# A two-layer decoder trunk in fp32: FFN in two parts with h kept in DRAM, and four gate and up groups with a fourth seven-product pair

## The chip, the cores and the metric

The kernel runs on one core of one Trainium2 chip. The metric is the device time of one execution in microseconds, the median of the runs. The engines are PE (matrix products), DVE (vector), ACT (scalar), POOL and SP; the last two mostly issue DMAs here, though POOL computes a little as well.

## What is computed

Two pre-norm residual layers on 256 rows of width 2048, in float32: the first mixes by sliding-window attention beside an mLSTM, the second by forgetting attention; each ends in a SwiGLU FFN of hidden width 5632. The change concerns the two FFNs alone.

```
def swiglu(xn, w_gate, w_up, w_down):
    return (jax.nn.silu(xn @ w_gate) * (xn @ w_up)) @ w_down

for layer in range(DEPTH):          # DEPTH = 2
    ...
    h = h + mix
    h = h + swiglu(rms_norm(h, norm_ffn[layer]), w_gate[layer], w_up[layer], w_down[layer])
return rms_norm(h, norm_final)
```

## The kernel before

**Products in three pieces.** Each float32 operand is split into a high and a low half of PE's faster 32-bit type. ACT casts the high half (L187, or L356 in `split_plain`), DVE subtracts it from the raw value for the low half (L188, L357). A product is three matmuls (`three`, L531 to L534, or `gemm`, L222 to L224): high by high, high by low, low by high. The right operand of a matmul is a 128x512 block of weights, the left a 128x128 block of the activations, which are kept turned (k on the partitions): `xh, xl` for the normed input, `mh, ml` for the FFN's middle values.

**Pairs of k tiles.** `pair_group` (L539) computes two 512-wide column blocks at once (gate and up, or two neighbouring blocks of down) over an order of k pairs. An entry (0, pair) is a plain pair: two matrices, two k tiles, two row tiles, three matmuls each. An entry (1, pair) is a block product in seven products instead of eight: DVE makes four differences of the weights (L607 to L610), they are split like weights, and the sums of the activations that go with them (`sums_of`, L263) have been made once beforehand. It holds four `prod` banks of PSUM beside the four plain `acc` banks; `combine` (L553) puts the four products together into the tile `c` (one buffer), to which the plain banks are added (L665). The two sets of banks come from two pools of four and change places from one group to the next (`par`).

**Orders.** `ORDER` makes pairs 1, 3 and 5 of the eight k pairs seven-product pairs. `HEAVY` makes it 1, 3, 5 and 7, and begins with pair 1; groups in `DENSE` use it, and `DENSE` is empty. The sums for pair 7 (`FOURTH`) are made all the same and lie in halves of `xh, xl` that seven-product pairs don't read, and in `x4`. `DOWN` has the orders for down, by number of k pairs.

**Stages.** FFN_HIDDEN is 11 groups of 512. `PARTS` = (0, 3, 7, 11) cuts them into three parts, of 3, 4 and 4 groups. In each part `ffn` (L637) runs its gate and up groups (silu at L667, the product with up at L669), and then the down products of that part's 12 or 16 k tiles, whose results are added to h in SBUF (L758, and `add_out`, L370). `mh, ml` hold the 16 k tiles of one part. In layer 1 the last part's second column half is computed plainly by `gemm`, with the final norm.

**Turning the middle values.** After a group, ACT separates c into 16-bit planes (L697) and SP turns them by transposing DMAs; `join`, which runs in place 5 or 6 of the next group's order, puts the planes together (L704), splits them and makes the sums for down. The last group of a part of three groups is turned by PE instead (L683), because its down run has no room to wait.

**What sets the order.** The tile framework schedules each engine's instructions from the order of emission, so neighbouring groups overlap. Converted weights go to a stock of eight buffer pairs (`slot`, L106), used in turn; raw weights come by SP's DMAs of 512 KB (L134) into four buffers for plain and four for seven-product pairs. h is a single buffer with the tag "h"; POOL issues the few DMAs that are not SP's.

Of the kernel before, what the change touches and what calls it, by code (L numbers as in the profile page):

```python
# [7 lines left out]
F32 = mybir.dt.float32  # L8
# [4 lines left out]
ALU = mybir.AluOpType  # L13
# [49 lines left out]
AHEAD_M = (1, 2)  # L63
PQ_AT = 6
TURNED_V = 2
PARTS = (0, 3, 7, 11)


def mixed_of(order):
# [6 lines left out]
def trunk(  # L76
# [459 lines left out]
    def bank(par, name):  # L536
        return pm.tile([P, NB], F32, tag="pm", name=name) if par else pa.tile([P, NB], F32, tag="acc", name=name)
# [99 lines left out]
    def ffn(layer, fp, sx, x4, sd, key, todo, idx_next=None, key_next=None, finish=None):  # L637
        r = rstd(key)

        def sums_x(pair):  # L640
# [2 lines left out]
            j = mixed_of(ORDER).index(pair)  # L643
            return four(sx[0], j), four(sx[1], j)

        for g0, g1 in zip(PARTS, PARTS[1:]):
            end = g1 == PARTS[-1]
            nk = 4 * (g1 - g0)
            order = DOWN[nk // 2]
            for g in range(g0, g1):  # L650
# [17 lines left out]
                for t in range(NT):  # L668
# [5 lines left out]
                        op0=ALU.mult,  # L674
                        op1=ALU.mult,
                    )
                if g == g1 - 1 and nk < 16:
                    for half in range(2):
                        pt = bank(par, "pf").rearrange("p (i q) -> p i q", i=2)
                        for i in range(2):  # L680
                            cs = (2 * half + i) * P
                            for t in range(NT):
                                nc.tensor.transpose(pt[:, i, t * P : (t + 1) * P], c[:, t, cs : cs + P], ident)  # L683
                        pair = 2 * (g - g0) + half
                        k = 2 * pair
                        split_plain(mh[:, k : k + 2, :], ml[:, k : k + 2, :], pt)
                        if pair in mixed_of(order):
                            j = mixed_of(order).index(pair)
                            sums_of(
                                fp, sd[0][:, j, :, :], sd[1][:, j, :, :], lambda full, pt=pt: nc.scalar.copy(full, pt)  # L690
                            )
# [8 lines left out]
                def join(c=c, turned=turned, g=g, g0=g0, order=order):  # L700
# [4 lines left out]
                    k = 4 * (g - g0)  # L705
                    split_plain(
                        mh[:, k : k + 4, :].rearrange("p k s -> p (k s)"), ml[:, k : k + 4, :].rearrange("p k s -> p (k s)"), ct
                    )
                    for half in range(2):
                        pair = 2 * (g - g0) + half  # L710
                        if pair in mixed_of(order):
                            j = mixed_of(order).index(pair)
                            sums_of(
                                fp,
                                sd[0][:, j, :, :],
                                sd[1][:, j, :, :],
                                None,
                                ct[:, half * 512 : (half + 1) * 512].rearrange("p (i t q) -> p i t q", i=2, t=NT),
                            )

                todo = [(MID if g < g1 - 1 else MID_DOWN, join)]

            def sums_d(pair, order=order):
                j = mixed_of(order).index(pair)
                return four(sd[0], j), four(sd[1], j)

            def close(acc, n):
                if not end:
                    add_out(acc, n)
                elif idx_next is None:  # L730
                    finish(acc, n, gf)
                else:
                    add_out(acc, n)
                    if n < 1:
                        todo.append((LATER_DOWN[n], split_turned(idx_next, n, *scrap(fp, n))))
                    else:
                        split_scaled(idx_next, n)
                    square_sum(key_next, n)

            gf = None  # L740
            wd = w_down[layer][4 * g0 * P : 4 * g1 * P, :]
            for n0 in (0, 2):
                if end and idx_next is None and n0 == 2:
                    for n in (2, 3):
                        acc = new_acc()
                        gemm(acc, m_of, wd, n * NB, NB, 0, nk, nk, skew=3 if n == 3 else 1, halved=n == 3)
# [6 lines left out]
                if end and idx_next is None:  # L753
                    gf = fp.tile([P, D], F32, tag="c", name="gf", bufs=1)
                    nc.gpsimd.dma_start(gf, norm_final.partition_broadcast(P))
                for t in range(NT):
                    o = h[:, t, n0 * NB : (n0 + 2) * NB]
                    nc.vector.tensor_tensor(  # L758
                        out=o, in0=c[:, 2 * t : 2 * t + 2, :].rearrange("p a n -> p (a n)"), in1=o, op=ALU.add
                    )  # L760
                for m in range(2):
                    close(plain[m], n0 + m)

    def close_layer(layer, w_out, idx, key, **rest):
        with tc.tile_pool(name=f"fp{layer}", bufs=2) as fp:
            nx = len(mixed_of(ORDER))
            nd = max(len(mixed_of(o)) for o in DOWN.values())
            sx = [fp.tile([P, nx, 4, P], F32R, name=f"sx{i}", bufs=1) for i in range(2)]
# [608 lines left out]
```

## Time and profile before

| | |
|---|---|
| runs | 2077.94, 2077.02, 2076.69 us, median 2077.02 |
| profiled execution | 2077.56 us, span 2075.9 us, clock 0.999 |
| PE | 2065.7 us busy, 9473 instructions |
| DVE | 1819.0 us busy, 2367 instructions |
| ACT | 1373.7 us busy |
| DMA | 209 GB/s on average, 408.68 MB read from HBM |
| first silu of layer 0, of layer 1 | at 365.4 us, at 1422.6 us |

Times in views of the trace are counted from the span's start. A busy row is the union of an engine's instructions; one that waits is not busy. In the groups' lists a line gives code line, engine, operation, out<-in and shape. In a list of waits a row names who waited, for whom, the total, the number of times and the longest.

### The profile page before, as it was taken

The numbers are of one execution on the slowest core, as the hardware profiler recorded it, in microseconds if no ns is written. First come the engines' busy times: TensorE is split into PE (matmuls) and PEld (weight loads), VectorE is DVE, ScalarE is ACT, GpSimd is POOL, SyncE is SP. The second block draws the span as 40 slices with busy tenths as digits, with TensorE's granted clock in tenths as the row PEclk, the third lists the DMA queues.
The fourth block names the chain that finished last, engine by engine and source line by source line (L and its number), as shares of the span: only waits on it lengthen the run. The fifth ranks groups of instructions, "written<-read, shape, count | busy, mean of one in ns | idle before, by whom it ended". The sixth has DMA issues, their size and how long they took to land.

```text
span 2075.9 us, 26965 instructions
## 1 busy us (share of the span) xinstructions
PE 2065.7 (100%) x9473; PEld 1715.1 (83%) x9473; DVE 1819.0 (88%) x2367; ACT 1373.7 (66%) x1744; POOL 44.6 (2%) x66
## 2 busy tenths in 40 slices
PE   9999999999999999999999999999999999999998
PEld 7878888888888888888888888888888888888886
DVE  6788769999999999999899688689999999999994
ACT  6777678664676656667676776687655666556763
POOL 1010000000000000000000001000000000000000
PEclk9999999999999999999999999999999999999999
DMA  8566577666677666766676776586756677667764
GB/s 292 169 216 192 188 244 238 206 219 196 210 223 224 193 208 217 222 204 183 206 213 209 231 201 183 155 268 217 233 187 218 209 217 224 202 195 225 206 196 141
DMA packets 309576, 434.88 MB, mean 209 GB/s; under 512 B 106412, under 2 KB 114624, under 8 KB 309312
## 3 DMA queue, kind: packets, MB, share of 16 engines
q1 hardware_dynamic: 307088, 426.27, 66.1%
q0 software_dynamic: 1632, 5.80, 0.8%
q8 instruction: 74, 1.21, 0.2%
q10 hardware_dynamic: 720, 1.09, 0.2%
q14 instruction: 62, 0.51, 0.1%
HBM read 408.68 MB, written 2.12 MB: 198 GB/s over the span
## 4 chain that ended last, share of the span: by engine, by line
PE 97%; DVE 1%; ACT 1%; issue 1%; DMA 0%; POOLq 0%; POOL 0%; ACTq 0%; DVEq 0%
PE acc L532 21%; PE acc L534 21%; PE acc L533 21%; PE acc L223 6%; PE acc L222 6%; PE acc L224 6%; PE prod L532 5%; PE prod L533 5%; PE prod L534 5%; PE p L386 1%; PE po L487 1%; ACT s L420 0%; PE po L488 0%; DVE lo L188 0%; DMA raw<-in_w_down_dram 0%
## 5 line engine op out<-in xcount | busy, mean ns | idle before, releaser
L188 DVE TENSOR_TENSOR lo<-raw,hi 128x1024 fp32r<-128x1024 f32 (+3 forms) x656 | 771.1, 1195 | 135.5 <-ACT hi L187 133.0
L187 ACT CAST hi<-raw 128x1024 fp32r<-128x1024 f32 (+3 forms) x656 | 661.7, 1027 | 341.2 <-PE acc L534 137.2
L533 PE MATMUL acc<-lo,xh 128*128 128x512 f32 x1320 | 514.0, 389 | 0.0
L534 PE MATMUL acc<-hi,xl 128*128 128x512 f32 x1320 | 511.4, 389 | 0.0
L532 PE MATMUL acc<-hi,xh 128*128 128x512 f32 x1320 | 506.2, 390 | 0.0
L534 PEld LDWEIGHTS acc<-hi,xl 128*128 128x128 f32 x1320 | 247.8, 188 | 51.6
L533 PEld LDWEIGHTS acc<-lo,xh 128*128 128x128 f32 x1320 | 247.8, 188 | 51.4 <-issue 0.2
L532 PEld LDWEIGHTS acc<-hi,xh 128*128 128x128 f32 x1320 | 247.7, 188 | 51.3 <-issue 0.2
L356 ACT CAST hi<-raw 128x512 fp32r<-128x512 f32 x204 | 166.9, 819 | 160.7 <-PE acc L534 83.6
L357 DVE TENSOR_TENSOR lo<-raw,hi 128x512 fp32r<-128x512 f32 x204 | 191.6, 939 | 11.4 <-ACT hi L356 10.4
L533 PE MATMUL acc<-lo,mh 128*128 128x512 f32 x466 | 181.0, 389 | 0.0
L534 PE MATMUL acc<-hi,ml 128*128 128x512 f32 x466 | 180.3, 389 | 0.0
L532 PE MATMUL acc<-hi,mh 128*128 128x512 f32 x466 | 176.2, 389 | 0.1
L356 ACT CAST hi<-t 128x1024 fp32r<-128x1024 f32 x95 | 100.0, 1053 | 63.9 <-PE acc L534 38.0
L357 DVE TENSOR_TENSOR lo<-t,hi 128x1024 fp32r<-128x1024 f32 x95 | 116.2, 1224 | 15.2 <-ACT hi L356 15.0
L223 PE MATMUL acc<-lo,mh 128*128 128x512 f32 (+1 forms) x322 | 126.3, 392 | 0.0
L222 PE MATMUL acc<-hi,mh 128*128 128x512 f32 (+1 forms) x322 | 125.8, 391 | 0.0
L224 PE MATMUL acc<-hi,ml 128*128 128x512 f32 (+1 forms) x322 | 123.7, 391 | 0.0
L532 PEld LDWEIGHTS acc<-hi,mh 128*128 128x128 f32 x466 | 87.5, 188 | 18.5 <-ACT hi L187 0.5
L534 PEld LDWEIGHTS acc<-hi,ml 128*128 128x128 f32 x466 | 87.5, 188 | 18.2
L533 PEld LDWEIGHTS acc<-lo,mh 128*128 128x128 f32 x466 | 87.4, 188 | 18.2
L223 PE MATMUL acc<-lo,xh 128*128 128x512 f32 (+3 forms) x288 | 100.0, 348 | 0.2 <-DVE lo L188 0.2
(356 smaller groups left out, 3174.7 us busy)
## 6 DMA issues: line engine op xcount, KB each, us to landing
raw<-in_w_gate_dram SPq DMA_DIRECT2D x176, 512.0 KB, 4.5
raw<-in_w_up_dram SPq DMA_DIRECT2D x176, 512.0 KB, 4.6
raw<-in_w_down_dram SPq DMA_DIRECT2D x176, 512.0 KB, 4.8
raw<-in_w_in_odd_dram SPq DMA_DIRECT2D x88, 512.0 KB, 5.3
raw<-in_w_in_even_dram SPq DMA_DIRECT2D x51, 512.0 KB, 5.1
raw<-in_w_out_even_dram SPq DMA_DIRECT2D x32, 512.0 KB, 5.2
raw<-in_w_out_odd_dram SPq DMA_DIRECT2D x32, 512.0 KB, 4.7
hr<-in_w_in_even_dram SPq DMA_DIRECT2D x12, 512.0 KB, 4.5
```

The lines of the kernel that those rows point to most:

```text
L187: latest[0] = nc.scalar.copy(hi[:, k, 0:n], raw[:, k, 0:n])
L188: nc.vector.tensor_tensor(out=lo[:, k, 0:n], in0=raw[:, k, 0:n], in1=hi[:, k, 0:n].bitcast(F32), op=ALU.subtract)
L222: nc.tensor.matmul(o, ah[:, ts], hi, start=(k == 0), stop=False)
L223: nc.tensor.matmul(o, ah[:, ts], lo, start=False, stop=False)
L224: nc.tensor.matmul(o, al[:, ts], hi, start=False, stop=(k == k_all - 1 and cs.stop == n))
L356: nc.scalar.copy(dst_h, src)
L357: nc.vector.tensor_tensor(out=dst_l, in0=src, in1=dst_h.bitcast(F32), op=ALU.subtract)
L386: nc.tensor.matmul(pq[j % 2][:, j // 2, :], q_of(j, b), k_of(j)[:, 0:cols], start=True, stop=True)
L487: nc.tensor.matmul(po, v_of(j, 0), tt[:, j, 0:2, :].rearrange("p c q -> p (c q)"), start=True, stop=False)
L532: nc.tensor.matmul(o, ah, hi, start=start, stop=False)
L533: nc.tensor.matmul(o, ah, lo, start=False, stop=False)
L534: nc.tensor.matmul(o, al, hi, start=False, stop=stop)
```

## The change

`PARTS` becomes (0, 6, 11): two parts of 6 and 5 groups, so down runs over 12 and 10 pairs, each order with four seven-product pairs (1, 3, 5, 7 and 1, 3, 5, 8). `DENSE` becomes (3, 5, 7, 9). The first part has 24 k tiles of middle values, eight more than `mh, ml` hold. They go where h lay: h is stored to a DRAM tile `kept` as ffn begins, the tile `more` takes its SBUF buffer, and the first part's down results are added to `kept` by accumulating DMAs from c, issued by POOL. When the second part begins, h is loaded back. The second part's four extra k tiles go into the buffers `sx0, sx1`, free by then. The sums of the fourth down pair lie in halves that are not read otherwise. All groups are turned by DMA, and L683 is gone. `par` now simply alternates.

```
-DENSE = ()
+NK2 = 8
+DENSE = (3, 5, 7, 9)
 DOWN = {
-    6: ((0, 0), (1, 1), (0, 2), (1, 3), (0, 4), (0, 5)),
-    8: ((0, 0), (1, 1), (0, 2), (1, 3), (0, 4), (1, 5), (0, 6), (0, 7)),
+    12: tuple((int(pair in (1, 3, 5, 7)), pair) for pair in range(12)),
+    10: tuple((int(pair in (1, 3, 5, 8)), pair) for pair in range(10)),
 }
+DOWN_FOURTH = {12: 7, 10: 8}
-PARTS = (0, 3, 7, 11)
+PARTS = (0, 6, 11)
...
+        nonlocal h
+        par = 1
+        kept = dp.tile([P, NT, D], F32, name=f"kept{layer}")
+        for cs in (slice(0, D // 2), slice(D // 2, D)):
+            nc.gpsimd.dma_start(kept[:, :, cs], h[:, :, cs])
+        over = None
+        def mid(k, n):
+            if k < KT:
+                return mh[:, k : k + n, :], ml[:, k : k + n, :]
+            return tuple(m[:, k - KT : k - KT + n, :] for m in over)
...
+            if end:
+                h = cp.tile([P, NT, D], F32, tag="h", name="h")
+                for cs in (slice(0, D // 2), slice(D // 2, D)):
+                    nc.gpsimd.dma_start(h[:, :, cs], kept[:, :, cs])
+            else:
+                more = cp.tile([P, 2, NK2, S], F32R, tag="h", name="more")
+                over = more[:, 0, :, :], more[:, 1, :, :]
+            def room_of(pair, order=order, fourth=fourth, end=end):
+                if pair != fourth:
+                    j = mixed_of(order).index(pair)
+                    return sd[0][:, j, :, :], sd[1][:, j, :, :]
+                if end:
+                    return tuple(m[:, 4:6, :].rearrange("p a (b q) -> p (a b) q", b=2) for m in over)
+                return mh[:, 2:15:4, P:S], ml[:, 2:15:4, P:S]
             for g in range(g0, g1):
-                par = (g1 - 1 - g) % 2
+                par = 1 - par
...
-                if g == g1 - 1 and nk < 16:
-                    for half in range(2):
-                        pt = bank(par, "pf").rearrange("p (i q) -> p i q", i=2)
...
-                                nc.tensor.transpose(pt[:, i, t * P : (t + 1) * P], c[:, t, cs : cs + P], ident)
...
-                    continue
...
+            if end:
+                over = [fp.tile([P, 6, S], F32R, tag=f"sx{i}", name=f"over{i}", bufs=1) for i in range(2)]
...
             for n0 in (0, 2):
...
+                par = 1 - par
                 plain, c = pair_group(
-                    fp, 1 - n0 // 2, m_of, sums_d, [(wd, n0 * NB), (wd, (n0 + 1) * NB)], order, todo
+                    fp, par, mid_of, sums_d, [(wd, n0 * NB), (wd, (n0 + 1) * NB)], order, todo
                 )
+                if not end:
+                    for m in range(2):
+                        for t in range(NT):
+                            o = c[:, 2 * t + m, :]
+                            nc.vector.tensor_tensor(out=o, in0=plain[m][t], in1=o, op=ALU.add)
+                    nc.gpsimd.dma_start(
+                        kept[:, :, n0 * NB : (n0 + 2) * NB],
+                        c.rearrange("p (t m) n -> p t (m n)", t=NT),
+                        accum_op=ALU.add,
+                    )
+                    continue
```

More of the change, by code (lines that the diff above doesn't have):

```diff
@@ L699, in ffn, with join @@
                         nc.sync.dma_start_transpose(turned[b][:, :, t, :], flat[:, b, t, :])
-                def join(c=c, turned=turned, g=g, g0=g0, order=order):
+                def join(c=c, turned=turned, k=4 * (g - g0), order=order, room_of=room_of):
                     ct = c[:, 0:2, :].rearrange("p a n -> p (a n)")
@@ L704, in join @@
                         nc.scalar.copy(cb[:, :, b], turned[b].rearrange("p k t q -> p (k t q)"))
[L705 to L708, printed above, removed]
+                    split_plain(*(m.rearrange("p k s -> p (k s)") for m in mid(k, 4)), ct)
                     for half in range(2):
-                        pair = 2 * (g - g0) + half
+                        pair = k // 2 + half
                         if pair in mixed_of(order):
-                            j = mixed_of(order).index(pair)
                             sums_of(
                                 fp,
-                                sd[0][:, j, :, :],
-                                sd[1][:, j, :, :],
+                                *room_of(pair),
                                 None,
@@ L721, in ffn, with sums_d @@
                 todo = [(MID if g < g1 - 1 else MID_DOWN, join)]
-            def sums_d(pair, order=order):
-                j = mixed_of(order).index(pair)
-                return four(sd[0], j), four(sd[1], j)
+            if end:
+                over = [fp.tile([P, 6, S], F32R, tag=f"sx{i}", name=f"over{i}", bufs=1) for i in range(2)]
+            def sums_d(pair, room_of=room_of):
+                return [[m[:, e, :] for e in range(4)] for m in room_of(pair)]
             def close(acc, n):
-                if not end:
-                    add_out(acc, n)
-                elif idx_next is None:
+                if idx_next is None:
                     finish(acc, n, gf)
-                else:
[L733 to L738, printed above, removed]
+                    return
+                add_out(acc, n)
+                if n < 1:
+                    todo.append((LATER_DOWN[n], split_turned(idx_next, n, *scrap(fp, n))))
+                else:
+                    split_scaled(idx_next, n)
+                square_sum(key_next, n)
             gf = None
```

22 lines of the change are left out of this document (7 added, 15 removed).

## The prediction

> **What bounds the kernel now.** I read the page's first two parts and its chain, then who waited for whom on PE, then the order of time around one part boundary, then busy times group by group.
>
> ```profile
> PE 2065.7 (100%) x9473; PEld 1715.1 (83%) x9473; DVE 1819.0 (88%) x2367; ACT 1373.7 (66%) x1744; POOL 44.6 (2%) x66
> ...
> DVE  6788769999999999999899688689999999999994
> ...
> PE 97%; DVE 1%; ACT 1%; issue 1%; DMA 0%; POOLq 0%; POOL 0%; ACTq 0%; DVEq 0%
> ```
> ```profile
> PE cold L170 <- POOL ones L167: 1.2, 1, 1.2
> PE acc L223 <- DVE lo L188: 0.2, 1, 0.2
> PE acc L222 <- ACT hi L785: 0.2, 1, 0.2
> ```
>
> The reader is to see that PE works for 2065.7 of 2075.9 us, that the chain that ended last is 97% PE, and that all its waits for other engines come to 1.6 us. So PE alone sets the time: an instruction taken from PE is worth its full pace, as long as the engines that feed it keep ahead. VectorE (DVE) is the one that may not: its digits stand at 9 in both FFNs (slices 6 to 17 and the last ten), where it makes the low halves of the weights and the differences for the seven-product pairs.
>
> **What one matmul is worth.** A busy PE row is no price, because matmuls overlap (389 ns each, by the groups). The price is the distance between starts. From the order of time on PE at the end of the first down run of layer 0:
>
> ```profile
> 455.68 0.39 PE L533 MATMUL acc<-lo,mh 128*128 128x512 f32 x1
> ...
> 460.44 0.39 PE L534 MATMUL acc<-hi,ml 128*128 128x512 f32 x1
> 460.67 0.38 PE L683 MATMUL pf<-ident,c 128*128 128x128 f32 x2
> 460.81 0.48 PE L532 MATMUL prod<-hi,mh 128*128 128x512 f32 x1
> 461.12 0.39 PE L533 MATMUL prod<-lo,mh 128*128 128x512 f32 x1
> ```
>
> Between the first two rows lie 21 steps: 4.76 / 21 = 0.2267 us per 128x512 matmul. From 460.67 to 461.12 stand two transposes and one matmul: (0.45 - 0.227) / 2 = 0.11 us per transpose.
>
> The Trainium skill (page "TensorE: Matmul & The Clock Gate", section "Back-to-back issue gap") gives about 131 ns per matmul of 512 columns in a stream of weight loads and matmuls. By that the 21 matmuls below would be worth 2.8 us; the trace shows 227 ns here, and the trace decides.
>
> **PE, counted.** A pair of k tiles costs 2 matrices x 2 k x 2 row tiles x 3 = 24 matmuls plainly and 7 x 3 = 21 as seven products. So each pair made a seven-product pair takes 3 matmuls away.
> - Gate and up: groups 3, 5, 7 and 9 take HEAVY, four such pairs for three: 4 x 3 = 12 matmuls fewer per layer, 24 in all.
> - Down, layer 0: before 2 column halves x (2 + 3 + 3) = 16 such pairs; after 2 x (4 + 4) = 16. Nothing.
> - Down, layer 1, where the last part's second half is plain in both: before 4 + 6 + 3 = 13, after 8 + 4 = 12. Three matmuls more.
> - The eight PE transposes at the end of the first part of each layer (L683) go; that group now takes the DMA turn that the others take. 16 transposes fewer.
>
> Sum: 21 x 0.2267 + 16 x 0.11 = 4.8 + 1.8 = 6.5 us. That is all PE can give; the boundaries that disappear held no idle PE to win back, as the waits above show. The built program's order on PE has the same counts (21 fewer 128x512, 16 fewer 128x128), so the change does what it says, and I give that rival nothing.
>
> **DVE, counted.** Its prices are again distances between starts, from the order of time in one stretch where DVE runs without a gap:
>
> ```profile
> 548.68 0.68 DVE L607 TENSOR_TENSOR t<-raw 128x512 f32<-128x512 f32 x1
> 549.28 0.69 DVE L608 TENSOR_TENSOR t<-raw 128x512 f32<-128x512 f32 x1
> 549.88 0.68 DVE L665 TENSOR_TENSOR c<-acc,c 128x512 f32<-128x512 f32 x1
> 550.49 1.22 DVE L357 TENSOR_TENSOR lo<-raw,hi 128x1024 fp32r<-128x1024 f32 x1
> 551.62 0.68 DVE L665 TENSOR_TENSOR c<-acc,c 128x512 f32<-128x512 f32 x1
> ```
>
> So 0.60 us for 512 columns and 1.13 us for 1024. A plain pair needs two low halves of 1024 (2.26 us); a seven-product pair needs three of 1024, one of 512 and four differences (3 x 1.13 + 5 x 0.60 = 6.39 us). Each pair turned costs DVE 4.1 us to save PE 0.68 us.
> - The four dense groups: + 16.5 us per layer.
> - Two down runs fewer per layer, each with its combine (0.60 + 0.60 + 1.13), two adds of c to h (2 x 1.13) and four of the accumulators (4 x 0.60): - 14 us. The two runs that stay in the first part lose the two adds to h, which the accumulating DMA now does: - 4.5 us.
> - Layer 1's lost down pair: - 4.1 us.
>
> Net per layer: -2 us and -6 us. DVE's total doesn't grow; it moves from the down runs into the dense groups. What counts is each stage against PE:
>
> ```profile
> core 0: us, PE busy (x) PEld busy (x) DVE busy (x) ACT busy (x) POOL busy (x), PEclk, DMA share, GB/s
> 365.40:406.30 40.90, 40.90 (x183) 33.84 (x182) 39.08 (x50) 28.18 (x32) 0.00 (x0) 1.00 0.65 208
> 406.30:447.10 40.80, 40.80 (x182) 33.78 (x181) 40.47 (x51) 29.18 (x32) 0.00 (x0) 1.00 0.72 230
> ...
> 592.90:634.20 41.30, 41.30 (x184) 34.21 (x183) 39.63 (x50) 28.27 (x32) 0.00 (x0) 1.00 0.70 216
> 634.20:675.20 41.00, 41.00 (x183) 33.94 (x182) 39.65 (x50) 28.27 (x32) 0.00 (x0) 1.00 0.71 219
> ...
> 675.20:799.60 124.40, 124.40 (x551) 103.00 (x550) 114.87 (x131) 71.42 (x78) 0.00 (x0) 1.00 0.65 207
> ```
>
> The windows run from one group's first silu (L667) to the next; the last holds one group and two down runs of eight pairs. In the later groups DVE has some 1.6 us to spare in 41.3; in group 2 (second row) only 0.3, and PE still loses nothing. The last window without a group (39.6 of 41.3) leaves two down runs with 75.3 us of DVE in 83.1: 3.9 us spare each.
> - A dense group: DVE 39.6 + 4.1 = 43.7 us, PE 41.3 - 0.7 = 40.6 us. **DVE is 3.1 us short.**
> - The group after it, in ORDER, returns 1.6 us. So over groups 3, 4, 5 the debt runs 3.1, 1.5, 4.6 us; over 7, 8, 9, 10 it runs 3.1, 1.5, 4.6, 3.0 us.
> - The down runs of twelve pairs that follow group 5: one more seven-product pair and three more plain pairs (6.4 + 6.8 us) less the adds to h (2.3 us): 37.6 + 10.9 = 48.5 us of DVE beside 41.5 + 93 x 0.2267 = 62.6 us of PE. 14 us spare each: any debt is paid there.
>
> So the question is whether DVE runs far enough ahead of PE to carry 4.6 us of debt. Who waited for whom in 593 to 675 us:
>
> ```profile
> ACT hi L356 <- PE acc L534: 10.2, 8, 1.7
> ...
> ACT hi L187 <- PE acc L534: 1.4, 4, 0.4
> ACT hi L187 <- PE prod L534: 1.0, 1, 1.0
> ```
>
> The conversions wait for PE to give back a buffer pair of the stock: they run ahead as far as the eight pairs reach. A plain pair takes two, a seven-product pair four, 22 for the eight pairs of a group, so eight buffer pairs hold about 2.9 k pairs, some 15 us of PE; with the k pair that PE is reading taken off (5 us) the lead is about 10 us, an estimate from these rows. That covers 4.6 us, but not by much at its lowest points: a seven-product pair wants four conversions in a burst, and group 3 comes soon after group 2, which left DVE 0.3 us. The nearest row for a stall where the lead has run out is the first part's boundary in before: the window
>
> ```profile
> 411.00:482.00 71.00, 70.89 (x317) 58.37 (x316) 69.55 (x85) 45.02 (x50) 0.00 (x0) 1.00 0.69 214
> ```
>
> lost 0.11 us of PE with DVE at 98%. Bounds for the eight dense groups: 0, and 8 x 3.1 = 25 us if no lead carried them. I take 1.2 us, 0.3 for each of the four in the first parts, near the low end because the row at 98% is that cheap.
>
> **What lies beside other work.** ACT gains one conversion of 1024 and one of 512 per dense group, at 28.3 busy of 41.3 us. SP gets four more transposing DMAs per layer. POOL's queue gets six DMAs of 1 MB per layer.
>
> ```profile
> L1147 POOL DMA_DIRECT2D h<-in_x_dram x4: 722/726/731, 221.5 to 223.7; - x4
> ```
> ```profile
> 329.44 0.69 POOL L254 TENSOR_TENSOR r<-tot,mhalf 128x2 f32<-128x2 f32 x1 [66.81 <-DVE tot L252]
> ```
> ```profile
> raw<-in_w_gate_dram SPq DMA_DIRECT2D x176, 512.0 KB, 4.5
> ...
> h<-in_x_dram POOLq DMA_DIRECT2D x4, 512.0 KB, 6.9
> ...
> turned<-c SPq DMA_TRANSPOSE x80, 2.5
> gf<-in_norm_final_dram POOLq DMA_DIRECT2D x1, 1024.0 KB, 8.1
> ```
>
> - The two stores of h stand ahead of r on POOL: 2 x 0.73 = 1.5 us later than 329.4, with the first silu at 364. Hidden. They bring 2 MB beside weights that arrive at 208 GB/s with the DMA engines 65% busy; the loads are issued ahead, and I cost a few us of later landing at nothing. If that cover is gone, it is up to 8.1 - 4.5 = 3.6 us once per layer, 7 us in all.
> - c of a first-part down run must stay until the accumulating DMA has read it. The next writer is the next combine: two thirds of a run later for the first (42 us), and after the seven-product pair in place 5 of group 6 for the second (about 33 us, less 4 for the adds). No row shows an accumulating DMA; the nearest is the plain 1 MB from POOL at 8.1 us. Between nothing and three times that it is hidden, and I take nothing. The reload of h has the whole second part before its first reader.
> - The four transposing DMAs (2.5 us) replace two PSUM conversions per layer and are hidden as in the other groups.
>
> **Sum.** Profiled execution: 2077.56 us, its span 2075.9 and 1.66 around it, which stays. 2077.56 - 6.5 + 1.2 = 2072.3. The median of the runs, 2077.02, is 0.5 lower, so **2071.7 us** for the median.
>
> **The rivals.** A measurement can tell about 0.2% here, 4.2 us: 2072.9 and 2081.2 are the bounds.
> - *The dips eat the gain* (no change). Each dense group stops PE for some 0.7 us, as much as it saves: only the transposes and a little remain, 2077.0 - 6.5 + 8 x 0.7 = 2076. For it: DVE over 40 us of 40.8 in group 2. Against: PE without a wait there.
> - *DVE becomes the bound* (slower). DVE works in order: an add that waits for PE's last matmul of a bank stops the conversions behind it, so the lead never builds up to what the buffers allow. From a lead under 3.1 us at the start of a dense group each pays the rest. In full: 2077.0 - 6.5 + 25 = 2095; it passes 2081.2 when the eight lose 1.35 us each. For it: DVE's nines, and HEAVY starts with a seven-product pair, whose bursts follow the adds of the group before. Against: the conversions' waits for buffers.
> - *The accumulating DMA holds c* (slower). From about 29 us in the second run it stops the combine, then the banks, then PE; at 40 us it costs 11 us per layer: 2077.0 - 5.3 + 22 = 2094. Beside it stands a rule of the Trainium skill (page "SBUF — State Buffer", section "SBUF: two separate sides"): a DMA issued from GpSimd can starve while VectorE runs two-port operations. The POOL rows above landed in 6.9 and 8.1 us; whether that holds beside FFN work no row of before shows.
>
> **Chances.** Forecast (stalls under 2.4 us, 2070.5 to 2072.9): 0.62. Dips eat the gain (2072.9 to 2081.2): 0.23. DVE the bound: 0.12. c held: 0.03. Faster 0.62, within 0.2% 0.23, slower 0.15. The range takes the first two and ends at their bounds: 2070.3 (all of the 6.5 us, and 0.2 of scatter) to 2081.
>
> **What would show it.** PE's count down by 37, its waits under 2 us, DVE busy 43 us of 41 in the windows of groups 3, 5, 7, 9 (that is, no idle) with the waits of conversions for PE gone there, and the down windows with DVE idle of some 10 us. Wrong would be PE waiting for lo (L190 there) or for a bank that an add holds in the dense groups, SP or ACT waiting on raw after the stores of h, or a combine that waits for a DMA.

## The result, and the profile after

The changed kernel takes 2087.8 us (median of four runs, 2086.5 to 2088.5) beside 2077.4 us of the kernel before (four runs, 2076.7 to 2077.9). The ratio is 1.0048, 95% interval 1.0034 to 1.0062: **slower by 10.4 us**, where 5.3 us less was forecast. The profiled execution took 2088.07 us, its span is 2086.3 us.

The page's counts of PE and DVE, DVE's digits and the chain, of the kernel after:

```profile
PE 2065.0 (99%) x9436; PEld 1708.4 (82%) x9436; DVE 1814.2 (87%) x2363; ACT 1389.2 (67%) x1760; POOL 53.5 (3%) x78
...
DVE  6788769999998899999799688589999987999984
...
PE 74%; DVE 12%; DMA 5%; ACT 4%; issue 4%; SPq 0%; ACTq 0%; POOLq 0%; POOL 0%; DVEq 0%
```

PE has the 37 instructions fewer that were counted, and its busy time hardly falls; the chain that was 97% PE is now 74% PE, with DVE, ACT and DMAs in it. The digits show where DVE works less: the 8s and 7s in slices 13 and 14, 33 and 34 lie where the first parts' down runs are now. Who PE waited for, after:

```profile
PE acc L535 <- DVE lo L190: 3.6, 5, 1.2
PE prod L534 <- ACT hi L358: 2.1, 3, 1.0
PE acc L534 <- ACT hi L189: 1.7, 3, 0.7
PE prod L534 <- DVE xl L364: 1.5, 1, 1.5
PE cold L172 <- POOL ones L169: 1.2, 1, 1.2
PE pt L291 <- issue: 1.2, 1, 1.2
PE acc L534 <- ACT c L557: 0.6, 1, 0.6
PE acc L534 <- DVE c L560: 0.5, 2, 0.3
```

Before it was 1.6 us in three rows. Now conversions (L189, L190, L358), the combine (L557, L560) and the next layer's input (L364) are late for PE. A list of waits shows only the part of a stop in which PE's modelled busy rows have run out. To count whole stops I take each distance between two neighbouring matmuls' starts, less the 0.2266 us of the steady pace, and add those over 0.05 us. By that count PE loses 11.3 us in before (its own start and the attention stages) and 27.8 us after: 16.5 us more, less the 6.5 us of work taken away, is 10.0 us of the 10.4 by which the span grew. By place, in us (a group's row goes from the first silu of the group before it to its own):

| place | before | after | parts alone | pair 8 to 7 | DVE relieved | five, stores by SP |
|---|---|---|---|---|---|---|
| layer 0: up to group 0's end | 0 | 1.4 | 1.3 | 1.7 | 2.3 | 0 |
| layer 0: groups 3, 5, 7, 9 | .6, 0, 0, 0 | 1.9, .9, 0, 3.2 | 0 | 1.9, .9, 0, 3.8 | 0 | 0 |
| layer 0: after group 10 | 0.1 | 4.8 | 3.2 | 1.2 | 3.2 | 0.2 |
| layer 1: up to group 0's end | 0 | 0.2 | 0.7 | 0 | 0.6 | 0 |
| layer 1: groups 3, 5, 7, 9 | .2, 0, 0, 0 | 2.4, .9, 0, 1.9 | 0 | 2.0, .9, 0, 1.9 | 0 | 0 |

The other groups lose nothing in any of these kernels. So the dense groups lose 11.2 us for the 5.4 us that they save (24 matmuls), the end of layer 0 loses 4.8 us, and the beginnings of the FFNs 1.6 us.

Group by group in layer 0, windows from one group's first silu (L701) to the next; columns as in the windows of before: length, then busy time (and count) of PE, PEld, DVE, ACT, POOL.

```profile
406.50:449.30 42.80, 42.80 (x190) 35.43 (x190) 40.72 (x52) 29.79 (x33) 0.00 (x0) 1.00 0.67 210
449.30:496.80 47.50, 46.56 (x203) 37.38 (x202) 46.26 (x59) 31.31 (x36) 0.00 (x0) 1.00 0.72 218
...
535.10:579.40 44.30, 43.69 (x193) 35.82 (x192) 43.64 (x52) 30.63 (x33) 0.00 (x0) 1.00 0.72 215
579.40:740.00 160.60, 160.60 (x710) 133.00 (x709) 139.58 (x156) 89.91 (x95) 3.78 (x4) 1.00 0.76 233
740.00:783.10 43.10, 43.10 (x191) 35.67 (x191) 41.11 (x53) 29.61 (x33) 0.00 (x0) 1.00 0.68 217
...
825.20:872.40 47.20, 44.83 (x196) 36.16 (x195) 45.89 (x58) 31.36 (x34) 0.00 (x0) 1.00 0.69 212
```

The first row is group 2; rows two, three and the last are groups 3, 5 and 9: DVE busy for 97 to 99% of them, and PE no longer for all. Group 7 (row five) comes behind the two down runs and group 6 (row four), in which DVE had 21 us to spare, and loses nothing. One stop closely, DVE and then PE in order of time near the end of group 9's window:

```profile
869.36 0.69 DVE L610 TENSOR_TENSOR t<-raw 128x512 f32<-128x512 f32 x1
869.96 1.22 DVE L190 TENSOR_TENSOR lo<-raw,hi 128x1024 fp32r<-128x1024 f32 x1
871.09 0.69 DVE L560 TENSOR_TENSOR c<-prod,c 128x512 f32<-128x512 f32 x1
```
```profile
869.62 0.39 PE L534 MATMUL acc<-hi,xh 128*128 128x512 f32 x1
871.24 0.50 PE L535 MATMUL acc<-lo,xh 128*128 128x512 f32 x1 [1.23 <-DVE lo L190]
```

The low half ends at 871.18, and the matmul that reads it starts at 871.24: there is no lead left. DVE had not stood still: before that row comes a difference for the next seven-product pair and, behind it, the combine. By the count of matmuls (2387 of the FFN are done there, and the groups up to 9 have 2334) PE is already in the first pairs of group 10: the debt of a dense group is paid in part by the group that follows.

### The profile page after: what moved, and what is told of

It is laid out like the page before. It is cut to its first block, busy times and chain, and to the rows that moved or that the text cites. A ratio compares the mean times of both kernels' runs of the same rounds, so it can differ in the third digit from the quotient of the medians.

```text
span 2086.3 us, 26854 instructions
## 1 busy us (share of the span) xinstructions
PE 2065.0 (99%) x9436; PEld 1708.4 (82%) x9436; DVE 1814.2 (87%) x2363; ACT 1389.2 (67%) x1760; POOL 53.5 (3%) x78
## 4 chain that ended last, share of the span: by engine, by line
PE 74%; DVE 12%; DMA 5%; ACT 4%; issue 4%; SPq 0%; ACTq 0%; POOLq 0%; POOL 0%; DVEq 0%
PE acc L535 16%; PE acc L536 16%; PE acc L534 16%; PE acc L224 4%; PE acc L225 4%; PE acc L226 4%; PE prod L534 4%; DVE lo L190 4%; PE prod L536 4%; PE prod L535 4%; DVE lo L359 2%; DMA raw<-in_w_up_dram 2%; ACT hi L189 1%; ACT box L324 1%; DMA raw<-in_w_gate_dram 1%
## 5 line engine op out<-in xcount | busy, mean ns | idle before, releaser
L189 ACT CAST hi<-raw 128x1024 fp32r<-128x1024 f32 (+3 forms) x649 | 654.5, 1027 | 407.8 <-PE acc L536 191.7
L190 DVE TENSOR_TENSOR lo<-raw,hi 128x1024 fp32r<-128x1024 f32 (+3 forms) x649 | 763.1, 1193 | 150.1 <-ACT hi L189 147.3
L535 PE MATMUL acc<-lo,xh 128*128 128x512 f32 x1272 | 495.7, 390 | 3.5 <-DVE lo L190 3.3
L534 PE MATMUL acc<-hi,xh 128*128 128x512 f32 x1272 | 478.6, 391 | 2.5 <-ACT hi L189 1.4
L358 ACT CAST hi<-raw 128x512 fp32r<-128x512 f32 (+1 forms) x218 | 176.9, 819 | 63.4 <-PE acc L536 43.1
L359 DVE TENSOR_TENSOR lo<-raw,hi 128x512 fp32r<-128x512 f32 (+1 forms) x218 | 203.3, 936 | 6.8 <-ACT hi L358 6.6
L358 ACT CAST hi<-t 128x1024 fp32r<-128x1024 f32 x102 | 107.2, 1051 | 71.7 <-PE prod L536 46.5
L225 PE MATMUL acc<-lo,mh 128*128 128x512 f32 x320 | 125.9, 394 | 0.0
L224 PE MATMUL acc<-hi,mh 128*128 128x512 f32 x320 | 125.4, 392 | 0.0
L226 PE MATMUL acc<-hi,ml 128*128 128x512 f32 x320 | 123.3, 392 | 0.0
L535 PE MATMUL acc<-lo,mh 128*128 128x512 f32 x302 | 117.4, 389 | 0.3 <-DVE lo L190 0.3
L536 PE MATMUL acc<-hi,ml 128*128 128x512 f32 x302 | 117.2, 389 | 0.0
L534 PE MATMUL acc<-hi,mh 128*128 128x512 f32 x302 | 112.6, 389 | 0.4 <-ACT hi L189 0.4
L226 PE MATMUL acc<-hi,xl 128*128 128x512 f32 (+3 forms) x288 | 98.9, 344 | 0.0
L224 PE MATMUL acc<-hi,xh 128*128 128x512 f32 (+3 forms) x288 | 96.5, 348 | 0.5 <-ACT hi L189 0.5
L612 DVE TENSOR_TENSOR raw<-raw 128x512 f32<-128x512 f32 x116 | 80.0, 689 | 0.7
```

The source lines that it names most:

```text
L189: latest[0] = nc.scalar.copy(hi[:, k, 0:n], raw[:, k, 0:n])
L190: nc.vector.tensor_tensor(out=lo[:, k, 0:n], in0=raw[:, k, 0:n], in1=hi[:, k, 0:n].bitcast(F32), op=ALU.subtract)
L224: nc.tensor.matmul(o, ah[:, ts], hi, start=(k == 0), stop=False)
L225: nc.tensor.matmul(o, ah[:, ts], lo, start=False, stop=False)
L226: nc.tensor.matmul(o, al[:, ts], hi, start=False, stop=(k == k_all - 1 and cs.stop == n))
L358: nc.scalar.copy(dst_h, src)
```

## The experiments

All times are medians; each is compared with the kernel before on the same chip (2077.4 to 2077.6 us throughout).

**1. The parts alone.** `DENSE = ()` in the changed kernel.

> The changed kernel with DENSE empty: two parts with h in DRAM, no dense gate and up group. Theory: PE loses time at three separate places, the dense groups (11 us in all for 5.4 us saved), the end of layer 0's FFN (4.8 us) and its beginning (1.3 us); so without the dense groups the loss there and the saving both go: 2087.8 - 11 + 5.4 = about 2082, PE without gaps in groups 3, 5, 7 and 9, the other two places as they are. Rival: the two parts themselves (the traffic of kept, the moved buffers) make the feeding engines late everywhere, dense or not: 2087.8 + 5.4 = 2093.

Measured: 2084.4 us, ratio 1.0029 [1.0017, 1.0041]; the profiled execution 2081.0, the fastest of its runs. No group loses anything (the table). So by the medians 3.4 us of the 10.4 are the dense groups', net of what they save (by the two profiled executions 7.1, by the stops 11.2 - 5.4 = 5.8), and the two parts cost time by themselves, at the beginning and the end of the FFN.

**2. The dense groups alone.** `DENSE = (3, 5, 7, 9)` in the kernel before.

> The kernel before with DENSE = (3, 5, 7, 9): three parts, h in SBUF, only the dense groups added. Theory (VectorE's debt in a dense group runs the lead out, whatever the parts): 2077.4 - 5.4 + 11 = about 2083, gaps of PE of 1 to 2 us near the end of each dense group. Rival (dense groups are harmless by themselves): 2077.4 - 5.4 = 2072.

Measured: 2091.2 us, ratio 1.0068 [1.0053, 1.0083], 8 us more than the theory's 2083. Its stops are 19.4 us longer than before's: 15.8 us stand in the dense groups with what follows them directly (5.8 and 6.0 in the two groups 5, where PE waits 2.5 and 2.9 us for the combine), and 4.0 us at the end of layer 0, with the down runs of before. So the dense groups cost more than they save without the parts, too; with the two parts they lose less, 11.2 us.

**3. The fourth pair of ten at 7.** In the runs of ten pairs, with the sums of pair 7 in dead halves of `mh, ml`. In layer 1 those halves are read by the plain second column half, so there a part of the products takes other values than the reference's.

```
-    10: tuple((int(pair in (1, 3, 5, 8)), pair) for pair in range(10)),
+    10: tuple((int(pair in (1, 3, 5, 7)), pair) for pair in range(10)),
```

> The changed kernel with the fourth seven-product pair of the ten-pair down order at pair 7 instead of 8, its sums in the dead halves of mh and ml. Theory (the 4.8 us at the end of layer 0 come from VectorE having the burst of pair 8 and the combine in the last two pairs of the last run, beside the scaling of the next layer's input): three plain or two plain pairs stand after it instead of one, 3 to 5 us less, 2083 to 2085. Rival (the end waits for h from DRAM, or for debt of group 9): no change, 2088.

Measured: 2086.3 us, ratio 1.0049 [1.0032, 1.0066], not to be told from the changed kernel by the runs; but by the stops the end of layer 0 falls from 4.8 to 1.2 us. Two places make up most of it. At 981.7 us PE waits 1.5 us for L364 (above), the low half of the next layer's input; in the changed kernel, DVE in order of time:

```profile
981.04 0.48 DVE L364 SCALAR_TENSOR_TENSOR xl<-pt,gT,xh 128x256 fp32r<-128x256 f32 x1 [0.32 <-ACT xh L363]
981.44 0.68 DVE L612 TENSOR_TENSOR raw<-raw 128x512 f32<-128x512 f32 x1
982.04 0.48 DVE L364 SCALAR_TENSOR_TENSOR xl<-pt,gT,xh 128x256 fp32r<-128x256 f32 x1
```

These L364 stand among the differences (L609 to L612) of pair 3 of the last run. With the pair at 7 they stand there as well (978.95 to 982.6 us), and PE waits 0.5 us instead of 1.5; why less was not separated. With the dense groups alone, which leave the down runs as they were, PE waits 2.9 us at this place, so the dense groups bring it, too. The second place is the run's end, DVE and then PE:

```profile
1013.61 1.22 DVE L561 TENSOR_TENSOR c<-prod,c 128x1024 f32<-128x1024 f32 x1
1014.87 2.36 DVE L783 TENSOR_TENSOR h<-c,h 128x1024 f32<-128x1024 f32 x2
1017.14 2.48 DVE L372 TENSOR_TENSOR h<-acc,h 128x512 f32<-128x512 f32 x4
```
```profile
1016.32 0.39 PE L536 MATMUL acc<-hi,over 128*128 128x512 f32 x1
1017.93 0.41 PE L291 MATMUL pt<-ident,h 128*128 128x128 f32 x2 [1.22 <-issue]
```

Behind the run's last product PE turns h (L291), to which L783 and L372 add; they stand behind the combine, and the combine behind the last seven-product pair. With that pair at 8 the first L372 starts 0.8 us behind the start of PE's last product; at 7 it starts 1.1 us ahead of it (1013.80 and 1014.89 us), and the stop of 1.4 us is gone. The parts alone and the run of experiment 7, with the pair at 8, have it, too (1.3 us).

**4 and 5. Two stores that did not move.** The stores of h were emitted later: ahead of group 3, and then in place 3 of group 2 behind a conversion.

> The changed kernel with the two stores of h issued before group 3 instead of at the beginning of the FFN. Theory (the gap of 1.4 us at 351 us in layer 0 comes from the stores making the turning DMAs of h land up to 7.2 us instead of 2.5 us after issue): the gap goes, 1.3 us less, 2086.5; the turning DMAs near 331 us land in 2.5 to 5 us as in before. Rival (the gap is the order's, not the transfers'): no change of the gap.

> The changed kernel with the two stores of h issued in place 3 of group 2 (held there behind a conversion), some 70 us and more later than now, away from the transposing DMAs of the layer's last stage. Theory A (the stores beside these DMAs delay SP's queue by 2.5 us and so the first group's weights): the stop of 1.3 us at 351.5 us of layer 0 goes (under 0.3 us there) and nothing comes in its place, time 1.3 us below the changed kernel's, about 2086.5. Rival B (the first group stops there for a reason of its own, since all kernels in two parts do it): the gap stays at 1.0 us or more. Rival C (the stores delay whatever they lie beside): the gap goes, and one of 1 us or more comes in group 2 or 3.

Measured: 2088.8 and 2088.9 us. Neither tells anything of the stores: in both traces POOL, which had nothing else to do, issued them at 281 and 329 us as ever; neither the place in the program nor the conversion, which is ACT's, held POOL back. Both are further runs of the changed kernel, in effect, with the same order on PE, DVE and ACT, and lie 1 us above it.

**6. Two plain pairs at the end of a dense group.**

```
-HEAVY = ((1, 1), (0, 0), (1, 3), (0, 2), (1, 5), (0, 4), (1, 7), (0, 6))
+HEAVY = ((1, 1), (0, 0), (1, 3), (0, 2), (1, 5), (1, 7), (0, 4), (0, 6))
```

> The changed kernel with one line changed: the order of the dense groups is (1,1),(0,0),(1,3),(0,2),(1,5),(1,7),(0,4),(0,6), the same four seven-product pairs, but two plain pairs behind the last of them instead of one. Theory A (VectorE's debt: 4.1 us more work per group for 0.68 us less on TensorE, and not enough conversions made ahead): the work is the same, so the dense groups still lose about as much as in the changed kernel (some 11 us in the eight, 1.4 us each), time 2085 to 2090. Rival B (the order: the last seven-product pair comes so late that the combine has no plain pairs to hide behind): the gaps at the end of dense groups shrink to under 0.5 us each, some 7 us in all, time 2079 to 2082.

Measured: 2103.1 us, ratio 1.0125 [1.0112, 1.0139]. Worse than either theory. Two bursts stand side by side now, and the combine, though two plain pairs cover it, is late as well (L557; 0.6 us in the changed kernel):

```profile
PE prod L534 <- ACT hi L358: 5.4, 9, 1.0
PE acc L534 <- ACT c L557: 4.4, 2, 2.2
PE prod L534 <- DVE xl L364: 3.7, 1, 3.7
```

Rival B is out: more room behind the last pair does not heal it. The waits move to the products of the seven-product pairs (L358) and to the groups behind the dense ones, 17 us of stops in all groups for 11.2. As I read it, order matters because a burst needs a lead that is there at that moment. Part of the time is a lower clock: behind the stops at 568 and 989 us the granted clock was 0.50 for 3.4 us.

**7. DVE relieved.** In dense groups the pairs 5 and 7 skip their four differences; the raw weights take their place, which leaves out that part of the computation.

```
+                    bare=(5, 7) if g in DENSE else (),
...
-            t4 = ra if halves else fp.tile([P, 2, NB], F32, tag="t4", name="t4", bufs=1)
+            t4 = rb if pair in bare else ra if halves else fp.tile([P, 2, NB], F32, tag="t4", name="t4", bufs=1)
...
+            if pair not in bare:
+                nc.vector.tensor_tensor(out=ta, in0=rb[:, 0, :], in1=ra[:, 0, :], op=ALU.subtract)
...
```

> The changed kernel, but in the dense groups the pairs 5 and 7 skip their four differences on VectorE (eight subtractions of 0.687 us, 5.5 us per dense group): the raw weights are split and multiplied in their place, so this leaves out a part of the computation, while TensorE, ScalarE and the DMAs do the same work in the same order. VectorE then has 38.2 us of work beside 40.6 us of TensorE in a dense group instead of 43.7. Theory A (VectorE's debt): the gaps in the eight dense groups go (11 us to under 2 us), time 2077 to 2080; what stays is the beginning of layer 0's FFN (1.3 us), the end of layer 0 (4.8 us). Rival B (order and place of the pairs, the combine at the end): most of the gaps stay, time 2084 to 2088.

Measured: 2076.5 us (ten runs, 2073.7 to 2080.5), ratio 0.9998 [0.9989, 1.0007]. With the same number of instructions on PE and ACT, 5.5 us less of DVE per dense group take 11.3 us away. Groups 3, 5, 7 and 9 in its windows:

```profile
450.20:492.50 42.30, 42.30 (x189) 35.01 (x188) 37.62 (x46) 29.41 (x33) 0.00 (x0) 1.00 0.73 212
...
535.80:574.10 38.30, 38.30 (x171) 31.71 (x170) 33.50 (x38) 27.66 (x31) 0.00 (x0) 1.00 0.66 214
737.90:779.70 41.80, 41.80 (x186) 34.59 (x185) 35.43 (x44) 29.52 (x34) 0.00 (x0) 1.00 0.68 226
...
820.30:861.10 40.80, 40.80 (x182) 33.78 (x181) 38.24 (x46) 28.73 (x32) 0.00 (x0) 1.00 0.70 233
```

PE is busy without a gap in each. So the work that the dense groups add on DVE is what they pay for; what stays (2.3 and 3.2 us in layer 0) are the beginning and the end. Two things changed with it that the run does not separate from DVE's time: conversions no longer wait for the differences, and from 460 us on the engines' order differs from the changed kernel's.

**8. The stores by SP.** In place 3 of group 2, in SP's order.

```
-                nc.gpsimd.dma_start(kept[:, :, cs], h[:, :, cs])
+                with tc.issue_after(loaded[0].ins):
+                    loaded[0] = nc.sync.dma_start(kept[:, :, cs], h[:, :, cs])
```

> The changed kernel with the two stores of h issued by SP instead of POOL, in SP's order behind the weights' loads of the middle of group 2 (about 425 us in layer 0 instead of 281 and 329). In the run before this one POOL issued them at 281 and 329 us as ever, so that run told nothing of the stores. Theory A (the stores beside the transposing DMAs make SP's queue late, and that stops the first group at 351 us): that stop of 1.0 to 1.3 us goes (under 0.3 us), first silu at 364 us as in the kernel before, time 1.3 us below the changed kernel's 2087.8, if nothing comes in its place in group 2. Rival B (the stop has another cause): it stays at 1.0 us or more, though the transposing DMAs land in 2.5 us again. Rival C: the stop goes, but the weights behind the stores in group 2 come late and one of 1 us or more stands there.

Measured: 2093.7 us, ratio 1.0079 [1.0066, 1.0093], a miss in the sum. The stop at 351 us is gone (theory A), but the dense groups now lose 19.5 us (2.8, 4.3, 0, 5.1 and 2.8, 2.3, 0, 2.2) instead of 11.2. The moved stores also made the scheduler order conversions and matmuls otherwise from group 2 on. How much of the 8 us is that order and how much the later weights (ACT waits 3.2 us for one of up in groups 2 and 3) was not separated. With the one debt the groups thus lose 11.2, 15.8, 17 and 19.5 us in four orders (the changed kernel, experiments 2, 6 and 8): without the debt there are no stops, but the order has a large part in their size.

**9 and 10. A version without dense groups.** Two parts, `DENSE = ()` and no sums for `FOURTH`; the runs of twelve with a fifth seven-product pair (9), its sums in those rooms; the fourth pair of ten at 7 in layer 0; first with the stores by POOL, then by SP.

```
+DENSE = ()
...
-    12: tuple((int(pair in (1, 3, 5, 7)), pair) for pair in range(12)),
+    12: tuple((int(pair in (1, 3, 5, 7, 9)), pair) for pair in range(12)),
...
+DOWN_0 = tuple((int(pair in (1, 3, 5, 7)), pair) for pair in range(10))
+FIFTH = 9
...
+            if end and layer == 0:
+                order, fourth = DOWN_0, 7
...
+                if pair == FIFTH:
+                    return rooms(xh), rooms(xl)
```

> What the first runs point to, put together: two parts as in the changed kernel, no dense groups (and the sums for their fourth pair not made), the stores of h in place 3 of group 2, the down runs of twelve pairs with a fifth seven-product pair (9; its sums lie where the sums of the dense groups' fourth pair lay), and in layer 0 the down runs of ten pairs with the fourth seven-product pair at 7 instead of 8. Counted from the kernel with the parts alone (2084.4 median, 2081.0 profiled): stores 1.3 us less, the end of layer 0 2 us less, four more seven-product pairs of 0.68 us, 2.7 us less. If the down runs have the VectorE time to spare that the windows show (10 us each), 2075 to 2079, beside 2077.4 of the kernel before; if a fifth pair makes a debt as the dense groups do, gaps of over 1 us each in the four runs, 2080 to 2085.

> The kernel with five seven-product pairs in the runs of twelve once more, unchanged, for a second profile of it. Its eleven runs lay between 2075.1 and 2082.8 us; the first profile was of the fastest. If the scatter is TensorE waiting, a profile of a slower execution shows stops that the first does not have, of the same sum as the difference in time; if it is spread over all matmuls (a longer time for each), the stops stay at 11 us and the matmuls are longer.

> The kernel with the parts alone, a fifth seven-product pair in the down runs of twelve and the fourth at 7 in layer 0's runs of ten, with its stores of h issued by SP in the middle of group 2. Its sister with the stores by POOL: 2079.05 median of runs from 2075.1 to 2082.8, though its profiled execution (2075.1) stops TensorE for only 11.3 us, 1 us more than the kernel before. If the early stores cause the scatter (they meet the transposing DMAs at another moment each time): median 2074 to 2076, runs within 2 us, faster than the kernel before. If they do not: 2077 to 2080 with the same scatter of some 8 us.

Measured: with POOL, which issued the stores at 281 and 328 us again, 2079.1 us (eleven runs, 2075.1 to 2082.8), ratio 1.0010 [1.0001, 1.0019]; the second profile, of an execution of 2078.35 us, shows stops of 3.7 us at layer 1's beginning (1390 to 1410 us) and 0.5 at layer 0's that the first profile, of 2075.10, does not have, and 0.6 instead of 1.2 us in layer 1's group 1. So the scatter is PE waiting, in the places that follow the early stores. With SP: **2073.2 us** (eleven runs, 2072.9 to 2074.2), ratio 0.9980 [0.9971, 0.9989]: faster than both kernels, and the scatter is 1.3 us. Its page and PE's waits:

```profile
PE 2060.5 (99%) x9448; PEld 1712.6 (83%) x9448; DVE 1795.8 (87%) x2339; ACT 1383.9 (67%) x1748; POOL 49.6 (2%) x74
...
PE 97%; DVE 1%; ACT 1%; issue 0%; DMA 0%; SPq 0%; POOLq 0%; POOL 0%; ACTq 0%; DVEq 0%
```
```profile
PE cold L174 <- POOL ones L171: 1.2, 1, 1.2
PE acc L226 <- ACT hi L191: 0.5, 1, 0.5
PE acc L227 <- DVE lo L192: 0.2, 1, 0.2
PE acc L226 <- ACT hi L824: 0.2, 1, 0.2
```

PE has 25 instructions fewer than before: 16 transposes and 9 matmuls (three seven-product pairs more in all), 3.8 us at the prediction's prices. The runs give 4.35. Of the 3.8 us the transposes are 1.8, and the pairs 2.0, which come where DVE has time: in the down runs.

What the stores did beside the transposing DMAs of the stage before, issues from 276 to 342 us, the changed kernel and then this one (KB each, median us from issue to landing):

```profile
kept<-h POOLq DMA_DIRECT2D x2, 1024.0 KB, 5.8
box<-box SPq DMA_TRANSPOSE x16, 3.3
```
```profile
box<-box SPq DMA_TRANSPOSE x16, 2.5
```

Single ones took up to 7.2 us beside a store (issued at 330.7 us); in before, without a store, those issued at 328.4 to 331.0 us took 5.0 to 3.5. That they make group 0's weights late is not shown: from 335 to 362 us ACT waits 3.5 us for these in the changed kernel and 3.6 us in before, where PE does not stop. What the runs show is that the stop goes when the stores move (experiments 8 and 10), though the first profile of experiment 9 has early stores and no stop; the way from one to the other stays open.

**11. One difference on POOL.** The changed kernel with stores by SP, the fourth pair at 7 in layer 0, and the second difference of each seven-product pair of the FFN on POOL.

```
-            nc.vector.tensor_tensor(out=tb, in0=rb[:, 1, :], in1=rb[:, 0, :], op=ALU.subtract)
+            (nc.vector if halves else nc.gpsimd).tensor_tensor(out=tb, in0=rb[:, 1, :], in1=rb[:, 0, :], op=ALU.subtract)
```

> What the theory of VectorE's debt asks for: the changed kernel with its dense groups, the stores of h by SP in the middle of group 2, the fourth seven-product pair of layer 0's runs of ten at 7, and one of the four differences of every seven-product pair in the FFN (the second, which no other difference reads) on POOL, which is idle there; its 128x512 selections took 1.5 to 1.8 us each in the changed kernel, so it can hold one per pair. VectorE loses 0.69 us per seven-product pair: 2.75 us in a dense group, 40.95 us of its work beside 40.6 us of TensorE's, and 2.1 us in each other group. Counted from the kernel with five seven-product pairs and its stores by SP (2073.2): four pairs fewer in the runs of twelve, +2.7; dense groups, -5.4; so 2070.5 if the dense groups stop TensorE by under 0.3 us each. Theory A (the debt): 2070 to 2073. Rival B (a difference on POOL comes late for the conversion behind it, or POOL and VectorE slow each other where both read SBUF): stops in all groups, also in those that had none, 2080 or more.

Measured: 2107.8 us, ratio 1.0144 [1.0127, 1.0161]: rival B. POOL's groups, DVE's, and PE's largest wait:

```profile
L611 POOL TENSOR_TENSOR t<-raw 128x512 f32<-128x512 f32 x102 | 357.5, 3505 | 1022.9 <-DVE lo L360 639.7 <-DVE raw L612 121.5 <-DMA raw<-in_w_down_dram 80.8
```
```profile
L360 DVE TENSOR_TENSOR lo<-raw,hi 128x1024 fp32r<-128x1024 f32 x102 | 135.3, 1327 | 4.8 <-ACT hi L359 4.7
...
L610 DVE TENSOR_TENSOR t<-raw 128x512 f32<-128x512 f32 x102 | 91.8, 900 | 3.5 <-DMA raw<-in_w_up_dram 1.8 <-issue 1.2 <-DVE more L360 0.3
```
```profile
PE prod L536 <- DVE lo L360: 12.7, 14, 1.9
```

The difference took 3.5 us on POOL, where DVE needs 0.69 us, and DVE's neighbour (L610) takes 0.90 us instead of 0.69. The theory of the debt is not touched by this; the remedy was wrong. The Trainium skill ("SBUF — State Buffer", section "SBUF: two separate sides") says that a VectorE operation with two SBUF inputs and a GpSimd operation that reads SBUF shut each other out for a whole instruction. That agrees with the two rows. The run does not separate this from POOL's own pace.

## Why the prediction was wrong, point by point

- **PE's 6.5 us: right.** 37 instructions fewer, and where no engine is late the saving arrives (the eleven runs of the version with the stores by SP).
- **DVE's debt: borne out.** 3.1 us per dense group was counted; relieving 5.5 us per group ended the stops, and group 7, which starts rested, carries its 3.1 us without a stop. The size itself was not measured.
- **The lead of 10 us: the step that failed.** I took it from the stock of eight buffer pairs, less the pair being read, and put the stalls at 1.2 us. They were 11.2 us. Matching each low half of before with the first matmul that reads it shows why (by order, since the trace does not name buffers, so the figures are near ones): in group 5 the median lead is some 9 us, as estimated, though one low half, which ends at 608.27 us, is read 4.9 us later; in groups 1 and 2, soon after the FFN's start, the median is 5 to 6 us and the smallest under 3 us. The stock says how far the conversions may run ahead, not how far they have come. In the changed kernel the smallest is under 1 us in groups 3, 5 (it starts with 1.5 us of debt by the prediction's own count) and 9, and over 4 us in group 7. The row at 98% that lost 0.11 us was no price for it: it stood at one moment, not at the end of a debt. One of the signs named did not come either: the conversions' waits for PE did not go in the dense groups but grew, to 10.4 us in group 3's window and 9.0 in group 9's (5.9 to 6.7 us in before's groups 2 and 4 to 6). So the conversions reach the stock's limit at one time of a group and have no lead at another; whether a larger stock would carry the bursts no run tried.
- **The rival that came.** "DVE becomes the bound" describes it: DVE in order, the lead too short, and each dense group but group 7 pays for the rest. It passed 2081.2 us at 1.35 us each; 11.2 / 8 is 1.4. It had 0.12. Its reason (the lead never builds up) fits in part: the conversions do reach the stock's limit, as said above.
- **The stores of h, "cost at nothing": wrong in size, with the price if the cover goes near enough.** 1.4 us in layer 0 and 0.2 in layer 1 of the profiled execution (up to 3.6 us per layer was the other end; the second profile of experiment 9 has 3.7 us in layer 1). With the stores by SP the median of the version without dense groups is 5.8 us lower, with another order of the engines from 400 us on. The later landing shows on the transposing DMAs, which I had not named; ACT's waits for the weights did not grow.
- **The end of layer 0: not foreseen.** 4.8 us. The move of the fourth pair to 8 in the runs of ten was priced on PE and DVE as a sum, but not by what stands behind it: the combine and the adds to h, for which the next layer's first transposes wait (1.4 us). The rest comes among the conversions of the next layer's input, where the dense groups alone lose 4.0 us, too.
- **The accumulating DMA: right, no engine that computes waits for it** (POOL's reload of h does, 32.6 us in the two layers, hidden). It lands in 15.2 us at the median (11.4 to 17.1), about twice the plain 8.1 us of the row of before, well inside the 29 us; POOL's r and the reload of h (9.9 us) are hidden too. Of the starving that the Trainium skill describes ("SBUF — State Buffer", section "SBUF: two separate sides") the stores show nothing: 5.8 us, with DVE busy for half of that time; whether it is part of the 15.2 us no run here separates.

```profile
kept<-c POOLq DMA_DIRECT2D x4, 1024.0 KB, 15.2
h<-kept POOLq DMA_DIRECT2D x4, 1024.0 KB, 9.9
```

- **DVE idle in the down windows: right**, 21 us in one group and two runs.

The sum as it came: 2077.6 - 6.5 + 11.2 (dense groups) + 4.8 (end of layer 0) + 1.6 (beginnings) - 0.8 (stops of before in those places) = 2087.9, beside 2088.07 measured.

## What to carry to other kernels

When work is moved off the bounding engine onto one that is 96% busy, measure how far ahead that engine's results are ready at their tightest point in each stage, from the trace; the buffers only give the most that it can be. Put such trades where the helper has time to spare (here the down runs), not where it has 1.6 us in 41. And look at what stands behind the place to which a burst moves, and at what a "free" transfer lies beside: here its early place made the runs scatter.

## What was not expected of the hardware

- Transposing DMAs of SBUF to SBUF, 2.5 us at the median, took up to 7.2 us beside a 1 MB store from POOL, and up to 5.0 us at the same place without it.
- In the run with the dense groups alone PE's stops had a second price. Its windows in layer 0, 636 to 644 us (the third number from the end is the granted clock):

```profile
636.00:640.00 4.00, 1.85 (x9) 1.19 (x7) 2.46 (x4) 2.10 (x2) 0.00 (x0) 1.00 1.00 358
640.00:644.00 4.00, 3.60 (x9) 2.85 (x10) 4.00 (x6) 0.86 (x1) 0.00 (x0) 0.58 0.34 92
```

  After a stretch in which PE worked for 1.85 us of 4, the granted clock was 0.58 in the next 4 us, and PE did 9 matmuls there instead of 18. PE's wait there was 2.5 us; the granted clock was 0.5 for 3.4 us from 640.7 us on, and again behind the wait of 2.9 us in layer 1 (from 1705.6 us).
- One 128x512 subtraction on POOL took 3.5 us beside a busy DVE, five times DVE's 0.69 us.
